# A two-layer hybrid backbone on one core: decay matrices made once per head, SiLU on ScalarE, z gates as a block, and the last weights before each residual norm taken token tile by token tile

## The chip, the cores and the metric

One core of one Trainium2 chip runs the whole program in one launch. The metric is the device time of an execution in microseconds (us). The kernel before takes 1237.73 us, the median of 3 runs (1231.84 to 1239.37).

## The reference, cut to what matters

Two layers act on 384 tokens (128 context tokens, 256 latent tokens of a grid 64 wide) with D = 1024 and 8 heads of 128. Layer 0 mixes tokens with a gated DeltaNet in both directions, layer 1 with HGRN2 in both directions; behind each mixer stand a residual RMS norm, a second norm and a squared-ReLU MLP. All weights are float32.

```python
# layer 0, per direction, chunks of c tokens
qkv = silu(token_conv(qkv, conv_w, grid))          # conv of 5 taps
q, k = l2_normalise(q), l2_normalise(k)
beta = sigmoid(braw); g = -exp(a_log) * softplus(araw + dt_bias)
g = cumsum(g)
decay = exp(where(causal, g[:, None] - g[None, :], -inf))
lower = (k * beta) @ k.T * decay * strict          # tmat = inverse of (1 + lower)
qk = q @ k.T * decay
u, w = tmat @ (v * beta), tmat @ (k * beta * exp(g))
v_new = u - w @ state; o = (q * exp(g)) @ state + qk @ v_new
o = rms_norm(o_fwd + o_bwd, onorm_g) * silu(z); mix = o @ w_out
# layer 1, per direction, chunks of c tokens
b = cumsum(log f); q_in = q * exp(b); k_out = k * exp(-b)
o = causal(q_in @ k_out.T) @ v + q_in @ state
# behind each mixer
x = x + gt1 * rms_norm(mix, g1)
h = rms_norm(x, g2) * (1 + sc2) + sh2
x = x + gt2 * rms_norm(square(relu(h @ w1)) @ w2, g3)
```

## The kernel before

**Tiling.** Tokens stand in three tiles of 128 (`NT` = 3, tile 0 is the context). A float32 product with weights is made of three products of halves: `split` (L898) turns a piece of weights `wr` into a high half `wh` (a cast on ScalarE) and a low half `wl` (a subtraction on VectorE), both of type fp32r, and `mm3` (L918) issues hi·hi, lo·hi and hi·lo. The activations are held transposed as `hhi` and `hlo`. PSUM has 8 banks; tiles named `pj`, `acc`, `pf`, `nat`, `pb`, `po`, `k`, `pad` share them.

**Order of the work.** The functions do not issue instructions; they hand each one to a `Planner` (L431 to L687) with a cost, the tiles that it reads and writes, and the name of its unit (`pl.unit`). The planner then runs a list schedule over PE, VectorE (DVE), ScalarE (ACT), GpSimd (POOL) and the SP queue, with a table of shifts per unit, numbers of buffers per pool and a cost for each form, and writes one fixed order per engine. Every DMA is issued from the SP queue, in the order so found; a DMA that must wait there holds those behind it.

**Stages.** In time: the start (adaLN of the first norm, and the projection of the first weights, `k`); the first mixer, `gdn` (L1236); its output projection `out_proj` (L1090) with the residual norm `postnorm` (L1065) and the next `prenorm` (L1040); `mlp` (L1125); the second mixer `hgrn` (L1605) with its `out_proj`; the second `mlp`. Beside them `ada` (L976) and `ada_rows` (L952) make the modulation vectors.

**First mixer.** `phase1` (L1385) makes, for a head, k by `conv` (L1295: copies, five taps on ScalarE and VectorE, a Tanh on ScalarE and two products on VectorE that make of it twice the SiLU), k·k, and the matrices `PU`. `inverse` (L1418) inverts the 64-token blocks of four heads: the 32-wide diagonal blocks go through DRAM (`du`, `dt`) to a layout in which 31 steps on VectorE solve them all together, and matmuls on quarters of the array (`merge`, L1450) put the rest together. `phase2` (L1488) makes q, v and the gate z of a head and then the outputs. `decay` (L1367) is called by both phases: for each token tile a mask by a 128x256 bf16 matmul with the identity (`maskb`, `identb`), two products of 6 rows (`LR`) on top, and an Exp on ScalarE into `dec`.

**Residual norms.** In `out_proj` the output weights come as four units of 1 MB, (half of the columns) x (half of the rows `kh`); for each unit a loop over three token tiles adds 12 matmuls to `acc`, and in the last unit `postnorm` of a tile follows its 12. In `mlp` the last group (g = 7) of `w2` (L1177) does the same with its two halves. `postnorm` squares both halves of `acc` on ScalarE, raises the sum to the power -0.5 on POOL (`rms`, L1030) and updates `x` on VectorE; `prenorm` squares `x` again, scales it to `xn`, transposes `xn` on PE (`pj`, line 814) and makes `hf`, `hhi` and `hlo`. The first weights of the MLP (`w1_rows`, L1151, PSUM tile `nat`) then run token tile by token tile.

**Second mixer.** In `head` (L1637), `intra` (L1672, called 24 times) fills a 128x256 PSUM tile with zeros by one matmul of `zerob` and then writes blocks into it: per direction one 64x64 product (`A64`), two 32x32 products (`A32`), four 32x32 products (`hQD`, `hKD`).

```python
PE.matmul(pat[:, :256], lhsT=zerob[:, :128], rhs=zerob[:, :256], start=True, stop=True, ...)
for e in range(2):
    PE.matmul(pat[j0:j0 + 64, ...], lhsT=A64k[:, e, :], rhs=A64q[:, e, :], ..., tile_position=(0, j0))
    for hb in range(2): ...   # A32, 32 wide
    for bb in range(4): ...   # KD, 32 wide
```

Of the kernel before, what the change touches and what calls it, by code (L numbers as in the profile page):

```python
# [8 lines left out]
F = mybir.dt.float32  # L9
# [8 lines left out]
D = 1024  # L18
# [6 lines left out]
C_ID, C_SEL, C_TF, C_TB, C_SF, C_SB, C_ONE = 0, 128, 144, 272, 400, 528, 656  # L25
C_HM = 784
# [17 lines left out]
SWITCH = 1036
TICK = 10240 / 3
WINDOW = 3446
SHIFT = {'aoh0': -1315,
 'aopn0': -1765,
 'aopn1': -753,
 'aopn2': 6,  # L50
 'aow0': -66,
 'aow1': 105,
 'aow2': 91,
 'aow3': 243,
 'aow:ld': -320,
# [132 lines left out]
 'hz2': 84,
 'hz3': -246,
 'hz4': -223,  # L190
 'hz5': -369,
 'hz6': -535,
 'hz7': -381,
 'hz:sp': 41,
 'inv0': 376,
 'inv1': 197,
 'k0': 142,
 'k1': 387,
 'k2': -103,
 'k3': -103,  # L200
 'k4': 118,
 'k5': 72,
 'k6': -159,
 'k7': -12,
 'k:ld': -168,
 'k:sp': -484,
 'kk0': -48,
 'kk1': 100,
 'kk2': 8,
 'kk3': -1,  # L210
 'kk4': -88,
 'kk5': 536,
 'kk6': -386,
 'kk7': 561,
 'q0': 108,
 'q1': 47,
 'q2': -283,
 'q3': -54,
 'q4': -177,
 'q5': 328,  # L220
 'q6': -392,
 'q7': 128,
 'q:ld': 78,
 'q:sp': -489,
 'st0': -1339,
 'st1': -1079,
 'st2': -2702,
 'st3': -192,
 'st4': -270,
 'st5': -1125,  # L230
 'st6': -78,
 'st7': -66,
 'v0': -96,
 'v1': -39,
 'v2': 161,
 'v3': -310,
 'v4': -183,
 'v5': 36,
 'v6': -268,
 'v7': -231,  # L240
 'v:ld': -23,
 'v:sp': -349,
 'x': -1361,
 'z0': -467,
 'z1': -85,
 'z2': 193,
 'z3': -435,
 'z4': 339,
 'z5': -273,
 'z6': -30,  # L250
 'z7': 234,
 'z:ld': -146,
 'z:sp': -378}
# [4 lines left out]
ADA = ((675, 63), (1031, 109), (1624, 175), (3306, 321), (4201, 189), (4487, 20), (5276, 1), (5517, 124),  # L258
 (4443, 58), (10707, 169))
BUFS = {'A32': 5,  # L260
 'A64': 7,
 'CR': 5,
 'LR': 3,
 'Zs': 8,
 'ab': 2,
 'acc': 8,
 'adw': 3,
 'am': 4,
 'ar': 7,
 'atm': 4,  # L270
 'att': 5,
 'av': 4,
 'avj': 3,
 'ax': 5,
 'c4': 4,
 'cacc': 3,
 'cbuf': 2,
 'crow': 3,
 'dec': 7,
 'e1': 6,  # L280
 'gate': 5,
 'gr': 5,
 'hE': 3,
 'hEn': 3,
 'hKD': 5,
 'hQD': 5,
 'hel': 7,
 'het': 5,
 'hf': 4,
 'hf0': 1,  # L290
 'hhi': 5,
 'hk': 5,
 'hlo': 8,
 'hsf': 4,
 'inv': 4,
 'k0': 6,
 'k2': 2,
 'kT': 4,
 'ktt': 3,
 'lbo': 5,  # L300
 'lhl': 3,
 'mh': 5,
 'ml': 4,
 'mr': 6,
 'nat': 6,
 'natr': 3,
 'of': 5,
 'ofl': 1,
 'oin': 5,
 'on': 6,  # L310
 'osb': 3,
 'pad': 5,
 'pb': 8,
 'pf': 4,
 'pj': 3,
 'pm': 4,
 'pnt': 3,
 'po': 5,
 'r': 6,
 'rstd': 7,  # L320
 's0': 7,
 's1': 2,
 'sf': 3,
 'sg': 4,
 'sqj': 6,
 'ss': 8,
# [1623 lines left out]
```

## Time and profile before

| | us |
|---|---|
| median of 3 runs | 1237.73 |
| lowest, highest run | 1231.84, 1239.37 |
| span of the profiled execution (first to last instruction) | 1238.8 |
| PE busy in it | 1196.9 |
| VectorE busy | 822.5 |
| ScalarE busy | 626.9 |
| GpSimd busy | 66.4 |

No time other than its span is given for the profiled execution; the span stands 1.1 us above the median. Busy times are sums over instructions of one engine; engines work beside each other. "Idle" of PE is the part of a stretch in which no matmul was in flight. The granted TensorE clock of the execution is 0.971 of full speed in the mean.

### The profile page before, as it was taken

The numbers are of one execution on the slowest core, as the hardware profiler recorded it, in microseconds if no ns is written. First come the engines' busy times: TensorE is split into PE (matmuls) and PEld (weight loads), VectorE is DVE, ScalarE is ACT, GpSimd is POOL, SyncE is SP. The second block draws the span as 40 slices with busy tenths as digits, with TensorE's granted clock in tenths as the row PEclk, the third lists the DMA queues.
The fourth block names the chain that finished last, engine by engine and source line by source line (L and its number), as shares of the span: only waits on it lengthen the run. The fifth ranks groups of instructions, "written<-read, shape, count | busy, mean of one in ns | idle before, by whom it ended". The sixth has DMA issues, their size and how long they took to land.

```text
span 1238.8 us, 20262 instructions
## 1 busy us (share of the span) xinstructions
PE 1196.9 (97%) x7840; PEld 1068.7 (86%) x7840; DVE 822.5 (66%) x1673; ACT 626.9 (51%) x1253; POOL 66.4 (5%) x165
## 2 busy tenths in 40 slices
PE   5999999999998999999998999999998999999997
PEld 3877798999887999999887999998976898998886
DVE  3487997947779999984439856677776963323434
ACT  3364445556646634453327764774665564443432
POOL 1112100000002000000002000000002000000000
PEclk9998996969998999999999999999999999999999
DMA  8864553413234666665336723443334353424322
GB/s 304 289 249 141 205 123 115 135 65 105 88 112 163 233 263 249 231 251 187 129 106 224 230 78 110 127 145 115 113 111 170 139 183 107 140 99 168 137 103 85
DMA packets 76613, 195.89 MB, mean 158 GB/s; under 512 B 24318, under 2 KB 44950, under 8 KB 64486
## 3 DMA queue, kind: packets, MB, share of 16 engines
q1 hardware_dynamic: 76518, 194.61, 45.8%
q8 instruction: 61, 1.00, 0.3%
q14 instruction: 34, 0.28, 0.1%
HBM read 185.31 MB, written 9.27 MB: 157 GB/s over the span
## 4 chain that ended last, share of the span: by engine, by line
PE 93%; DMA 2%; ACT 2%; DVE 1%; POOL 1%; issue 1%; SPq 0%; POOLq 0%; DVEq 0%; ACTq 0%
PE pj L809 35%; PE acc L809 26%; PE pb L809 14%; PE pf L809 8%; PE nat L809 3%; PE po L809 2%; PE pb L814 2%; PE pad L809 2%; PE k L809 1%; DMA wr<-in_gk_dram 1%; DMA cst<-in_consts_dram 1%; POOL rstd L725 1%; DVE hf L736 1%; DMA x<-in_x_sample_dram 1%; ACT xn L774 0%
## 5 line engine op out<-in xcount | busy, mean ns | idle before, releaser
L725 DVE TENSOR_TENSOR wl<-wr,wh 128x1024 fp32r<-128x1024 f32 (+2 forms) x228 | 266.5, 1171 | 241.3 <-ACT wh L779 236.3
L779 ACT CAST wh<-wr 128x1024 fp32r<-128x1024 f32 (+2 forms) x228 | 229.8, 1010 | 385.5 <-PE acc L809 187.7
L809 PE MATMUL pj<-hhi,wh 128*128 128x384 f32 x800 | 270.4, 343 | 1.1 <-ACT hhi L779 1.1
L809 PE MATMUL pj<-hlo,wh 128*128 128x384 f32 x800 | 269.3, 342 | 0.1
L809 PE MATMUL pj<-hhi,wl 128*128 128x384 f32 x800 | 268.2, 341 | 0.0
L809 PEld LDWEIGHTS pj<-hhi,wh 128*128 128x128 f32 x800 | 150.9, 189 | 6.0 <-issue 1.6
L809 PEld LDWEIGHTS pj<-hhi,wl 128*128 128x128 f32 x800 | 150.9, 189 | 3.5 <-DVE cacc L730 0.4
L809 PEld LDWEIGHTS pj<-hlo,wh 128*128 128x128 f32 x800 | 151.0, 189 | 2.7 <-DVE hlo L725 0.3
L809 PE MATMUL acc<-wl,mh 128*128 128x512 f32 x384 | 149.6, 390 | 0.0
L809 PE MATMUL acc<-wh,ml 128*128 128x512 f32 x384 | 148.9, 390 | 0.0
L809 PE MATMUL acc<-wh,mh 128*128 128x512 f32 x384 | 141.7, 391 | 0.0
L730 DVE SCALAR_TENSOR_TENSOR avj<-av,cb 128x1024 bf16<-128x1024 f32 x112 | 134.1, 1219 | 3.2 <-DMA av<-in_wv_dram 2.8
L809 PEld LDWEIGHTS acc<-wh,ml 128*128 128x128 f32 x384 | 72.1, 188 | 14.5
L809 PEld LDWEIGHTS acc<-wl,mh 128*128 128x128 f32 x384 | 72.1, 188 | 14.3
L809 PEld LDWEIGHTS acc<-wh,mh 128*128 128x128 f32 x384 | 71.7, 188 | 13.4
L809 PE MATMUL pf<-wh,hhi 128*128 128x384 f32 x192 | 65.5, 344 | 2.8 <-ACT hhi L779 2.8
L809 PE MATMUL pf<-wl,hhi 128*128 128x384 f32 x192 | 66.1, 344 | 0.0
L809 PE MATMUL pf<-wh,hlo 128*128 128x384 f32 x192 | 65.3, 342 | 0.6 <-DVE hlo L725 0.6
L730 DVE SCALAR_TENSOR_TENSOR cacc<-cb,cw,cacc 128x392 f32<-128x392 f32 x96 | 58.1, 617 | 0.5 <-ACT cacc L774 0.2
L809 PE MATMUL pad<-ar,csil 128*32 128x256 f32 x320 | 31.7, 431 | 13.3 <-DVE csil L740 8.9
L774 ACT ACTIVATE hE<-pb 128x512 f32<-128x512 f32 x48 | 28.9, 603 | 23.1 <-PE pb L809 19.5
L809 PEld LDWEIGHTS pf<-wh,hhi 128*128 128x128 f32 x192 | 36.1, 188 | 4.3 <-ACT hhi L779 3.5
(255 smaller groups left out, 2004.7 us busy)
## 6 DMA issues: line engine op xcount, KB each, us to landing
wr<-in_w_dram SPq DMA_DIRECT2D x64, 1024.0 KB
av<-in_wv_dram SPq DMA_DIRECT2D x56, 512.0 KB
ar<-in_wa_dram SPq DMA_DIRECT2D x40, 512.0 KB
wr<-in_gq_dram SPq DMA_DIRECT2D x14, 1024.0 KB
wr<-in_hfi_dram SPq DMA_DIRECT2D x16, 768.0 KB
wr<-in_hqz_dram SPq DMA_DIRECT2D x8, 1024.0 KB
wr<-in_gout_dram SPq DMA_DIRECT2D x4, 1024.0 KB
wr<-in_hout_dram SPq DMA_DIRECT2D x4, 1024.0 KB
```

The lines of the kernel that those rows point to most:

```text
L725: self._go(lambda: self.r.tensor_tensor(fix(out), fix(in0), fix(in1), op), _n(out), [out], [in0, in1], rate, base=base)
L730: self._go(lambda: self.r.scalar_tensor_tensor(fix(out), fix(in0), fix(scalar), fix(in1), op0, op1, **{k: fix(v) for k, v in kw.items()}), ...
L736: self._go(lambda: self.r.tensor_scalar(*[fix(x) for x in args]), _n(out), [out], [in0, s1, s2], rate, base=None if self.e == "V" else 160 ...
L774: self.pl.add("S", lambda: self.r.activation(fix(out), fix(in_), func, **{k: fix(v) for k, v in kw.items()}), cost, w, [x for x in (in_, b ...
L779: self.pl.add("S", lambda: self.r.copy(fix(out), fix(in_)), cost, [out], [in_])
L809: self.pl.add("PE", lambda: self.r.matmul(fix(out), lhsT=fix(lhsT), rhs=fix(rhs), start=start() if callable(start) else start, stop=stop, ...
L814: self.pl.add("PE", lambda: self.r.transpose(fix(out), fix(in_), fix(ident)), 108.0, [out], [in_, ident], kind="tr")
```

## The change

1. **Decays once.** `decay` of a head runs once, into a tile of all three token tiles, and is stored to DRAM (`dd`). `phase1` of heads 4 to 7 reads it back as `dre`, `phase2` of all heads as `att`, where one product of 768 columns replaces three of 256.
2. **SiLU on ScalarE** in `conv` and for z in the first mixer, in place of Tanh and products on VectorE; the constants of the norms lose their factor 4.
3. **z gates as a block.** The weights `gq` are packed anew (k of heads 4 to 7, all z, then q and v per head); the eight z blocks run ahead of `phase2`, each stored to `zd` and read back (`zl`) where a head ends.
4. **Last weights by token tile.** In `out_proj` and in the last group of `mlp` (and for head 0 of the second mixer) both last units are split first, four pieces resident at once (`split4`, the fourth in the extra tiles `xh`, `xl`), and each token tile then takes its 24 matmuls in a row.
5. **`intra` 32 wide.** Four zero matmuls of 32x96 that cover the part above the diagonal blocks, all products 32 columns wide, each on its own quarter of the array's columns.
6. **`inverse`**: other layouts of `du` and `dt`, so that 24 transposes of 32x32 blocks become 4 large ones and there are fewer DMAs, with 24 more small ScalarE copies.
7. The small inputs come in one packed DMA (`sml`), `cst` in one, states in one DMA for both directions.
8. The planner's costs, buffer numbers and shifts are other numbers.

```diff
-        def decay(h, after):
-            dts = []
+        def decay(h):
+            pl.unit(f"d{h}")
+            e = tl("L3", "dec", 3, [128, NT, 2, 128])
             for n in range(NT):
                 px = pb()
-                e = tl("L1", "dec", 3, [128, 256])
...
-                S.activation(e, px[:, :256], AF.Exp)
-                dts.append(e)
-            return dts
+                S.activation(e[:, n].rearrange("p d t -> p (d t)"), px[:, :256], AF.Exp)
+            DM.dma_start(out=dd[h], in_=e.rearrange("p n d t -> p (n d t)"))
+            return e
+        def gate(h, p):
+            zs = tl("L1", "zs", ZS, [128, T])
+            S.activation(zs, p, AF.Silu)
+            DM.dma_start(out=zd[h], in_=zs)
...
-            t = tl("L1", "th", 2, [128, 392])
-            S.activation(t, acc, AF.Tanh, scale=0.5)
-            V.scalar_tensor_tensor(out[:, 0:128], t[:, 0:128], 1.0, acc[:, 0:128], ALU.add, ALU.mult)
-            V.scalar_tensor_tensor(out[:, 128:384].rearrange("p (r c) -> p r c", r=4),
...
+            S.activation(out[:, 0:128], acc[:, 0:128], AF.Silu)
+            S.activation(out[:, 128:384].rearrange("p (r c) -> p r c", r=4), sub(acc, 130, [[66, 4], [1, 64]]),
+                         AF.Silu)
...
-            dec = decay(h, qT)
             pkq = pb()
-            att = tl("L3", "att", 2, [128, NT, 2, 128])
+            att = decay_of(h, "att")
...
+        dts = [decay(h) for h in range(4)]
         for h in range(4):
             pl.unit(f"k{h}")
-            phase1(h, k0[1 + h])
+            phase1(h, k0[1 + h], dts[h])
...
+        for h in range(H):
+            pl.unit(f"z{h}")
+            gate(h, get(4 + h))
         for h in range(H):
-            phase2(h, get, 4 + 3 * h)
+            phase2(h, get, 12 + 2 * h)
```

```diff
+        pl.unit(f"{u}ow2")
+        pcs = split4([load(w[2 + kh], 4) for kh in range(2)], [128, 2, 512])
+        for n in range(NT):
+            pl.unit(f"{u}ow2")
+            pst[n][1] = ps("acc", 6)
+            for k in range(KC):
+                hi, lo = pcs[k // 2]
+                mm3(pst[n][1], hT["hi"][k][:, tsl[n]], hT["lo"][k][:, tsl[n]], hi[:, k % 2, :], lo[:, k % 2, :],
+                    k == 0, k == KC - 1)
+            pl.unit(f"{u}opn{n}")
+            postnorm(n, pst[n], x[n], gate)
...
+                for bb in range(4):
+                    PE.matmul(pat[32 * bb:32 * bb + 32, 32 * bb + 32:32 * bb + 128], lhsT=zerob[:, :32],
+                              rhs=zerob[:, :96], start=True, stop=True, tile_position=(0, 32 * bb),
+                              skip_group_check=True, after=[KD])
+                jobs = []
+                for e in range(2):
+                    j0, i0 = 64 * (1 - e), 64 * e
+                    for c in range(2):
+                        jobs.append((j0 + 32 * c, e, i0, 64, A64k[:, e, 32 * c:32 * c + 32], A64q[:, e, :]))
```

**How the order moves.** PE, one `intra` of a later head; `hQD`, `hKD`, `A` are the operands, `pb` the PSUM tile. Before:

```order
L809 LDWEIGHTS zerob
L809 MATMUL pb_7512<-zerob 128x256
L809 MATMUL pb_7512<-A_1527_7483,A_1528_7487 64x64
L809 MATMUL pb_7512<-A_1529_7490,A_1530_7493 32x32 x2
L809 MATMUL pb_7512<-hQD_7497,hKD_7503 32x32 x4
```

The last three rows stand there once more for the other direction. After the change:

```order
L926 MATMUL pb_7151<-A_1424_7132,A_1425_7137 32x64 x4
L926 MATMUL pb_7151<-A_1426_7139,A_1427_7146 32x32 x4
L926 MATMUL pb_7144<-vtt_6925,het_7108 128x128
L926 MATMUL pb_7164<-vtt_6925,het_7108 128x128 x2
L926 LDWEIGHTS zerob
L926 MATMUL pb_7151<-zerob 32x96
...
L926 MATMUL pb_7151<-hQD_7149,hKD_7162 32x32 x8
```

The 64-wide rows are gone and the zeros stand four times (the middle ones are left out); an `intra` is now mostly two visits to the narrow shape with other work between them, 47 in all for 24 calls.

PE, the residual norm behind the first mixer; `acc` takes output weights, `pj<-...xn` are the transposes of `prenorm`, `nat` the first MLP products. Before, `xn_4607`, `xn_4634` and `xn_4676` are token tiles 0, 1 and 2:

```order
L809 MATMUL acc_4526<-wh_4534,hlo_4011 128x512
L814 MATMUL pj_4643<-cst,xn_4607 128x128 x4
L814 MATMUL pj_4653<-cst,xn_4607 128x128 x4
L809 MATMUL nat_4686<-wh_4655,hhi_4680 128x256
L814 MATMUL pj_4691<-cst,xn_4634 128x128 x4
L814 MATMUL pj_4707<-cst,xn_4634 128x128 x4
L814 MATMUL pj_4718<-cst,xn_4676 128x128 x4
L814 MATMUL pj_4726<-cst,xn_4676 128x128 x4
L809 MATMUL nat_4686<-wl_4714,hhi_4680 128x256
```

After, they are `xn_4356`, `xn_4433` and `xn_4490`:

```order
L926 MATMUL acc_4382<-xh_4305,hlo_3975 128x512
L932 MATMUL pj_4468<-sml,xn_4433 128x128 x4
L926 MATMUL nat_4494<-wh_4418,hhi_4426 128x256
L926 MATMUL nat_4494<-wl_4428,hhi_4426 128x256
L926 MATMUL nat_4494<-wh_4418,hlo_4442 128x256
L932 MATMUL pj_4508<-sml,xn_4490 128x128 x4
L932 MATMUL pj_4514<-sml,xn_4356 128x128 x4
L932 MATMUL pj_4527<-sml,xn_4433 128x128 x4
L932 MATMUL pj_4536<-sml,xn_4490 128x128 x4
```

The first transposes of tile 0 and the first three `nat` products have moved up among the `acc` products of tile 2; behind the last `acc` product three `nat` products stand ahead of the first transposes of tile 2, and the second halves of tiles 0 and 1 stand behind those.

The SP queue in the first mixer after the change, where `dd` and `zd` are the new DRAM tiles and `wr` is a unit of weights (before, no row of this kind stands there but for `du` and `wr`):

```order
L943 DMA dre_1249<-dd 128x768
L943 DMA dre_1257<-dd 128x768
L943 DMA dre_1316<-dd 128x768
L943 DMA inv_1321<-du_89 96x1024
L943 DMA wr_1327<-in_gq_dram 128x2048
L943 DMA dre_1359<-dd 128x768
L943 DMA zd<-zs_1350 128x384
L943 DMA att_1388<-dd 128x768
```

Over the whole program the SP queue has 404 rows where it had 431, and 36 of them are the new stores and read-backs (8 `dd`, 8 `zd`, 4 `dre`, 8 `att`, 8 `zl`). Matmuls per kind: `LR` 96 to 48, `maskb` 48 to 24, `zerob` 24 of 256 columns to 96 of 96 columns; products of `acc`, `pj`, `pf`, `nat` are as many as before. VectorE has 1561 rows before and 1466 after, ScalarE 1107 and 1131, with five more table loads.

## Rows read from the trace of the kernel before

**Rows 1.** The page, busy time, share of the span and instructions of each engine.
```profile
PE 1196.9 (97%) x7840; PEld 1068.7 (86%) x7840; DVE 822.5 (66%) x1673; ACT 626.9 (51%) x1253; POOL 66.4 (5%) x165
```

**Rows 2.** The page, chain of work that ended last, by engine.
```profile
PE 93%; DMA 2%; ACT 2%; DVE 1%; POOL 1%; issue 1%; SPq 0%; POOLq 0%; DVEq 0%; ACTq 0%
```

**Rows 3.** Windows by stage: us, busy by engine, granted clock, DMA share, GB/s.
```profile
0.00:62.00 62.00, 46.80 (x315) 35.39 (x315) 23.95 (x62) 20.99 (x41) 7.04 (x23) 0.97 0.87 297
62.00:376.50 314.50, 312.67 (x2470) 271.70 (x2469) 245.39 (x657) 171.96 (x453) 28.66 (x79) 0.92 0.42 137
376.50:394.50 18.00, 12.55 (x69) 10.94 (x69) 17.11 (x34) 12.66 (x30) 4.70 (x10) 0.81 0.09 32
...
652.90:668.00 15.10, 9.98 (x47) 7.43 (x46) 14.10 (x30) 14.22 (x37) 7.78 (x15) 0.89 0.68 225
...
951.00:975.00 24.00, 16.55 (x99) 15.09 (x98) 22.29 (x42) 14.95 (x37) 6.45 (x14) 0.93 0.37 137
```

**Rows 4.** Waits of PE: waiting <- waited for: us in total, times, longest.
```profile
PE pj L814 <- DVE xn L736: 10.4, 6, 5.0
```

**Rows 5.** PE timeline of one head's decays: start, length, instruction.
```profile
90.76 0.27 PE L809 MATMUL pb<-maskb,identb 128*128 128x256 bf16 x1
...
91.17 0.28 PE L809 MATMUL pb<-maskb,identb 128*128 128x256 bf16 x1
```

**Rows 6.** Lines of PE by form: count | busy, mean ns | idle before.
```profile
L809 PE MATMUL pb<-maskb,identb 128*128 128x256 bf16 x48 | 13.9, 289 | 0.1
```

**Rows 7.** PE timeline of one `intra` of the second mixer.
```profile
716.97 0.28 PE L809 MATMUL pb<-zerob 128*128 128x256 bf16 x1
717.19 0.48 PE L809 MATMUL pb<-A,A 128*64 128x64 f32 x4
717.46 0.23 PE L809 MATMUL pb<-hQD,hKD 128*32 128x32 f32 x2
...
717.69 0.48 PE L809 MATMUL pb<-A,A 128*64 128x64 f32 x4
...
718.20 0.49 PE L809 MATMUL po<-s,hQD 128*128 128x128 f32 x2
```

**Rows 8.** PE timeline behind the first mixer; in brackets the idle time before.
```profile
375.90 0.39 PE L809 MATMUL acc<-wl,hhi 128*128 128x512 f32 x1
376.13 0.39 PE L809 MATMUL acc<-wh,hlo 128*128 128x512 f32 x1
377.94 1.11 PE L814 MATMUL pj<-cst,xn 128*128 128x128 f32 x8 [1.42 <-DVE xn L736]
381.74 0.58 PE L809 MATMUL nat<-wh,hhi 128*128 128x256 f32 x1 [2.69 <-ACT hhi L779]
...
386.67 0.56 PE L809 MATMUL nat<-wl,hhi 128*128 128x256 f32 x1
```

**Rows 9.** Timelines of ACT, DVE and POOL in the same stretch.
```profile
376.95 0.58 ACT L774 ACTIVATE sqj<-acc 128x512 bf16<-128x512 f32 x1
...
375.54 1.41 DVE L730 SCALAR_TENSOR_TENSOR x<-pnt,rstd,x 128x512 f32<-128x512 f32 x2 [0.29 <-POOL rstd L725]
...
384.51 0.88 DVE L736 TENSOR_SCALAR xn<-x,rstd 128x512 f32<-128x512 f32 x2 [0.44 <-POOL rstd L725]
...
377.89 0.43 POOL L725 TENSOR_TENSOR rstd<-ss 128x1 f32<-128x1 f32 x1
378.40 0.55 POOL L725 TENSOR_TENSOR rstd<-rstd,nhalf 128x1 f32<-128x1 f32 x1
```

**Rows 10.** Windows in the first mixer where the granted clock is low.
```profile
183.00:206.00 23.00, 22.24 (x316) 20.60 (x314) 17.30 (x50) 10.95 (x26) 1.08 (x6) 0.57 0.52 152
247.00:268.00 21.00, 20.05 (x263) 19.21 (x264) 6.47 (x16) 8.31 (x20) 0.14 (x2) 0.51 0.28 99
```

**Rows 11.** Waits of the SP queue: us in total, times, longest.
```profile
SPq L825 <- DVE wl L725: 563.1, 91, 19.1
...
SPq L825 <- DMA od<-of: 7.6, 6, 1.5
```

More of the change, by code (lines that the diff above doesn't have):

```diff
@@ new lines @@
+M_CC, M_ID, M_SEL, M_C0, M_DT, M_CW, M_OG, M_ADB, M_LG = 0, 16, 144, 146, 170, 172, 292, 294, 406
+M_COLS = 438
+RESERVE = {'A32': 26,
+ 'A64': 73,
+ 'CR': 13,
+ 'HC': 4,
+ 'LR': 2,
+ 'PU': 0,
+ 'T64': 7,
+ 'Zs': 28,
+ 'ab': 18,
+ 'acc': 1,
+ 'adw': 2,
+ 'am': 35,
+ 'ar': 2,
+ 'atm': 54,
+ 'att': 19,
+ 'av': 2,
+ 'avj': 2,
+ 'ax': 5,
+ 'c1': 40,
+ 'cacc': 0,
+ 'cb': 2,
+ 'cbuf': 3,
+ 'crow': 58,
+ 'cvec': 2,
+ 'dec': 22,
+ 'dre': 11,
+ 'e1': 29,
+ 'gate': 13,
+ 'gp': 13,
+ 'gr': 16,
+ 'hE': 7,
+ 'hEn': 10,
+ 'hKD': 7,
+ 'hQD': 9,
+ 'hel': 65,
+ 'het': 1,
+ 'hf': 8,
+ 'hf0': 3,
+ 'hhi': 20,
+ 'hk': 10,
+ 'hlo': 9,
+ 'hsf': 11,
+ 'inv': 30,
+ 'iv': 21,
+ 'k0': 7,
+ 'k2': 0,
+ 'kT': 37,
+ 'ktt': 0,
+ 'lbo': 2,
+ 'lhl': 17,
+ 'mh': 16,
+ 'ml': 31,
+ 'mr': 13,
+ 'mst': 23,
+ 'nat': 4,
+ 'natr': 21,
+ 'of': 0,
+ 'ofl': 0,
+ 'oin': 47,
+ 'on': 60,
+ 'ors': 11,
+ 'osb': 0,
+ 'pad': 2,
+ 'pb': 2,
+ 'pf': 1,
+ 'pj': 2,
+ 'pm': 5,
+ 'pnt': 5,
+ 'po': 3,
+ 'qT': 0,
+ 'r': 36,
+ 'rstd': 30,
+ 'rsu': 34,
+ 's0': 4,
+ 's1': 68,
+ 'sf': 0,
+ 'sg': 11,
+ 'sqj': 17,
+ 'ss': 24,
+ 'ss2': 34,
+ 'sso': 48,
+ 'ssq': 45,
+ 'swt': 2,
+ 'tb': 3,
+ 'th': 16,
+ 'vT': 0,
+ 'vtt': 2,
+ 'w': 62,
+ 'w2': 70,
+ 'wh': 0,
+ 'wl': 0,
+ 'wr': 22,
+ 'x': 22,
+ 'xh': 13,
+ 'xl': 13,
+ 'xn': 25,
+ 'zl': 1,
+ 'zs': 2}
@@ L295 @@
+ 'gp': 4,
+ 'gr': 8,
+ 'hE': 4,
+ 'hEn': 8,
+ 'hKD': 7,
+ 'hQD': 7,
+ 'hel': 7,
+ 'het': 4,
+ 'hf': 8,
+ 'hf0': 2,
+ 'hhi': 3,
+ 'hk': 6,
+ 'hlo': 6,
+ 'hsf': 2,
  'inv': 4,
- 'k0': 6,
+ 'iv': 6,
+ 'k0': 9,
  'k2': 2,
[L298 to L305, printed above, removed]
+ 'kT': 6,
+ 'ktt': 8,
+ 'lbo': 6,
+ 'lhl': 7,
+ 'mh': 6,
+ 'ml': 5,
+ 'mr': 3,
+ 'mst': 4,
+ 'nat': 5,
  'natr': 3,
- 'of': 5,
- 'ofl': 1,
- 'oin': 5,
+ 'of': 6,
+ 'ofl': 2,
+ 'oin': 6,
  'on': 6,
- 'osb': 3,
@@ L455, in place, with add @@
         self.nplace += 1
-    def add(self, eng, call, cost, writes, reads, func=None, dma=None, kind=None, grid=None, rows=1.0):
+    def add(self, eng, call, cost, writes, reads, func=None, dma=None, kind=None, grid=None, rows=1.0, geo=None):
         op = Op()
@@ L537, in run @@
         dma_free = 0.0
+        lanes = []
         actset = None
@@ L1596, in gdn @@
         get = blocks(a["gq"])
+        for h in range(4, 8):
+            decay(h)
         for h in range(4, 8):
```

907 lines of the change are left out of this document (461 added, 446 removed).

## The prediction

> **What bounds the kernel now.** I read the page first. PE is busy 1196.9 us, 97% of the span, VectorE 66%, ScalarE 51% [rows 1], and the chain that ended last is PE for 93% of the span [rows 2]. So only two kinds of saving count: time in which PE works (or switches) and time in which PE has nothing. The windows by stage show where the second kind is [rows 3]: 15.2 us in the start (62.00 less 46.80), 1.8 in the whole first mixer (314.50 less 312.67), and 5.45, 5.12 and 7.45 us, 18.0 together, behind the first mixer, behind the first MLP's end and behind the second mixer. The waits of PE put 10.4 us in six waits on `xn` of VectorE, the input of the transposes in those norms [rows 4]. In the first mixer VectorE is busy 245 us of 314.5, but PE hardly waits there, so work taken from VectorE alone buys nothing in that stage. The granted clock is another matter: 0.92 in the mean there, against 1.00 later; two stretches of 44 us together stand near 0.5, the lower of the two levels (1.2 of 2.4 GHz), although PE is busy through 42 of them [rows 10].
>
> **Part 1, the decays.** One tile of decays starts at 90.76 and the next at 91.17 [rows 5]: 0.41 to 0.42 us of PE for the mask and its two small products. There are 48 such tiles [rows 6], 24 go: 24 x 0.42 = **-10.1 us**, all of it PE time in a stage with no idle time to spare. Bounds: -7 (half of the masks' busy 13.9 us [rows 6], if the small products hide wholly) and -13 (24 x 0.55, mask 0.27 and products 0.28 one behind the other).
> What comes in their place is DMA: 8 stores and 12 read-backs of 393 KB, and for z 8 stores and 8 read-backs of 197 KB. At 137 GB/s and a DMA share of 0.42 [rows 3], the stage has room; 11 MB is some 80 us of the present rate spread over 314 us. I cost it at nothing on the path; what hides it is that the order issues the first read-backs well before the heads that use them. If that cover is gone it is the rival on the slower side below.
>
> **Part 2, `intra`.** One call runs from 716.97 to 718.20, 1.23 us [rows 7]. In it the zeros take 0.22 (to 717.19), each 64-wide round 0.27 or so (717.19 to 717.46), each group of 32-wide products 0.23 (717.46 to 717.69), and round and group come twice. After the change no shape alternates: one round of A products on four quarters in place of two (0.27), the eight diagonal products and the zeros in some 0.25, since a whole group of ten short records takes 0.23 with the switch to the next shape in it, and one more switch because the call now makes two visits, some 0.12 by half of such a group. That is 0.65 us: 1.23 - 0.65 = 0.58, times 24 calls = **-13.9 us**. Bounds: -17 if a call is one visit (0.12 less each), and +3 if nothing runs side by side (20 instructions at 0.07, a quarter of a 64-wide round, are 1.40 us).
> The page "TensorEngine Tiling (Array Packing)" of the Trainium skill, section Instruction Overhead, speaks against this part: each matmul has an overhead of about 60 cycles, so that splitting what is short already gains little. At 25 ns (60 cycles at 2.4 GHz) the 36 passes of the 16 products and four zeros would take 0.9 us by an estimate from that page, and the part would be worth 8 us. The group of ten records in 0.23 us shows less than that per record, so I stay with the rows; what would follow is the first rival.
>
> **Part 3, last weights by token tile.** Before, behind the first mixer, the last `acc` product starts at 376.13, the transposes run in pieces from 377.94, and steady `nat` products start at 386.67 only [rows 8]. With 12 products each, the three tiles' postnorms come 2.8 us apart and share ScalarE, VectorE and POOL, so that tile 2's `xn` is scaled at 384.51 [rows 9], 8.4 us after the last product starts. A product starts 0.23 behind the one before (375.90, 376.13). After the change each tile has 24 of them, so tiles come 5.5 us apart and tiles 0 and 1 are through when tile 2 ends; its chain runs alone. From [rows 9] it has: `sqj` 0.58 and its accumulator read, some 0.8; POOL's sum and power 0.43 + 0.55, 1.0; two `x` updates 1.4; the second square of `x` 0.8; POOL again 1.0; half of `xn` 0.45: **5.4 us**. The order shows that PE still stops for it: behind the last `acc` product there are only four transposes and three `nat` products (about 0.8 us), then the transposes of tile 2, and the second halves of tiles 0 and 1 behind them. So the stall shrinks by 8.4 - 5.4 = 3.0 us and does not go. Three places: **-9 us**. Bounds: 0, if the new order makes the wait as long by other means, and -20, the idle time of 18.0 and some fill, if the wait were gone. The end of the second MLP gains nothing: there only tile 2's chain counts, and it stands behind the last product as before.
>
> **Part 4, at about nothing.** SiLU and the bulk transposes take some 30 us from VectorE and add small ScalarE copies and five table loads; PE hardly waits for either engine in that stage and ScalarE is busy 172 of 314.5 us [rows 3]: 0, bounds -2 and +3. The order has some 20 more switches of PE to the shape of the adaLN products; at 0.1 us each: **+2**. The start: thirteen small DMAs fewer, but some transfers moved ahead in a stretch whose DMA share is 0.87: 0, bounds -4 and +4.
>
> **Sum.** 1238.8 - 10.1 - 13.9 - 9 + 2 = 1207.8 us of span. The span of the profiled execution is all that is given of it, and it stands 1.1 above the median of the runs, so the forecast is **1206.5 us**, 2.5% less. Its own range, from the bounds taken halfway, is 1195 to 1217.
>
> **Rivals.**
> First, short products gain little: `intra` is limited by instructions and not by shapes, so that part brings 0 to -8 us. For it: each record has some fixed cost, and there are now more rows. Against it: ten records in 0.23 us [rows 7]. The time is 1206.5 + 10 = 1217.
> Second, the stalls at the norms nearly vanish (-20 in place of -9), because VectorE and ScalarE have no more splits to do there and the wait on `xn` is the only long one [rows 4]. Against it: the order keeps tile 2 ahead of work that is ready. The time is 1195.
> Third, the clock: a part of the 44 us near 0.5 comes back up, as the small products of the decays, which are bf16 with 6 rows, leave the mixer and the z blocks, long runs of 384 columns, fill other places. They lose 20 us (23 x 0.43 and 21 x 0.49); two thirds of it are 13: 1193. Against it: the same z blocks then no longer stand between the chains of `phase2`, so stretches may fall that were at full clock; I hold both about as likely, and the other sign is in the upper range.
> Fourth, slower: the SP queue. It issues in one order and stops for a DMA that waits. A store that was read back has cost 7.6 us in six waits, 1.27 each [rows 11]; 36 new DMAs of this kind at 1.27 are 46 us of holding, in a stage where the queue already brings weights behind waits for `wl`, 563.1 us in all. If it falls into the order badly, the weight unit that stands behind is late and PE starves: 1206.5 + 46 = 1252. It decides when the hold is longer than PE can work on what is resident, two units of two blocks each. Against it: PE has waited for no weights in this mixer (1.8 us idle of 314.5), and the stores stand well ahead of most read-backs.
> The page "DMA: Bandwidth & Descriptors" of the Trainium skill, section Latency and other measured facts, names a fixed cost of about 2 us for a DMA. By it the 36 would hold for 72 us, an estimate, where the row gives 46; both weigh for this rival, and neither says how much of it reaches PE.
>
> **How the numbers follow.** Forecast 0.47, first rival 0.17, second 0.16, third 0.11, fourth 0.09. A measurement of this kernel can tell about 1% from no change, so faster means under 1225.4 and slower over 1250.1. The forecast, the second and third rival are faster with nearly all of their weight (0.71 of 0.74), of the first 0.12 of 0.17; the fourth is half slower and half between, since a part of the hold may be hidden. That gives 0.83 faster, 0.12 same, 0.05 slower. The range, with 1 in 10 left out at each side: 1178 (second and third together, and the lower bounds of parts 1 and 2) to 1231 (the first rival with no gain at the norms and something of the fourth).
>
> **What would show it.** In the profile of the changed kernel: `maskb` x24 and the first mixer's stage about 10 us shorter, at a like clock; one `intra` at 0.65 us of PE in its two visits, and the second mixer's stage about 14 us shorter; from the last `acc` product to the first transposes of tile 2 some 5 to 6 us, with PE's waits on `xn` still there but fewer; the tail as before. The forecast is wrong if PE waits on `wh` or `wl` in the first mixer with the SP queue held by `dre` or `att`, if the short products take 0.07 each one after the other, or if the mean granted clock of the first mixer moves by more than 0.02.

## The result, and the profile after

The changed kernel takes 1250.38 us in the median of 4 runs (1248.31 to 1252.60) against 1238.18 beside it: a ratio of 1.0113 (95% interval [1.0081, 1.0144], as in the brackets below), slower by 1.1%. The forecast was 1206.5 with a range up to 1231, so it was wrong in sign, by 44 us. The profiled execution has a span of 1249.1 us.

The page of the kernel after, busy times and the chain of waits by engine:

```profile
PE 1195.8 (96%) x7936; PEld 1054.9 (84%) x7936; DVE 796.9 (64%) x1578; ACT 635.0 (51%) x1282; POOL 66.0 (5%) x156
...
PE 80%; DVE 7%; ACT 6%; DMA 4%; issue 2%; POOL 1%; SPq 0%; DVEq 0%; POOLq 0%; ACTq 0%
```

VectorE lost 26 us, as meant, and PE's busy time is 1.1 us less than in [rows 1], where the forecast took some 24 us of work from it. PE's share of the chain fell from 93% [rows 2] to 80%: VectorE, ScalarE and DMA now end waits that count. The windows by stage of the kernel after (columns as in [rows 3]) show where:

```profile
0.00:67.00 67.00, 54.12 (x371) 38.57 (x372) 30.61 (x69) 27.43 (x51) 7.21 (x22) 1.00 0.93 341
67.00:378.80 311.80, 295.77 (x2349) 257.41 (x2348) 236.07 (x600) 183.30 (x485) 27.75 (x76) 0.93 0.56 179
378.80:390.80 12.00, 5.94 (x26) 4.99 (x26) 10.47 (x20) 7.08 (x18) 4.47 (x7) 0.67 0.70 242
390.80:662.10 271.30, 271.30 (x1402) 244.92 (x1401) 174.75 (x249) 117.30 (x180) 3.56 (x10) 1.00 0.52 181
...
676.80:959.30 282.50, 280.32 (x2316) 250.27 (x2314) 217.74 (x486) 167.69 (x340) 12.47 (x21) 1.00 0.41 142
```

The same stages of the kernel before, cut at the same events:

```profile
0.00:61.70 61.70, 46.50 (x314) 35.33 (x315) 23.95 (x62) 20.69 (x41) 7.04 (x23) 0.97 0.87 296
61.70:376.30 314.60, 312.77 (x2472) 271.76 (x2470) 245.19 (x657) 172.06 (x452) 28.54 (x78) 0.92 0.42 137
376.30:387.00 10.70, 5.91 (x27) 4.50 (x27) 9.81 (x20) 10.29 (x27) 4.82 (x11) 0.70 0.07 29
387.00:655.30 268.30, 267.65 (x1404) 243.63 (x1402) 196.24 (x291) 116.75 (x178) 2.20 (x8) 1.00 0.56 205
...
666.80:952.70 285.90, 285.31 (x2169) 260.96 (x2167) 204.68 (x455) 171.26 (x334) 8.97 (x16) 1.00 0.42 136
```

In the first mixer PE is busy 17.0 us less, but idle for 16.0 us where it was 1.8. A second profile of the kernel after (run 2 below) has it idle for 9.4 us, at a lower clock:

```profile
66.50:376.60 310.10, 300.74 (x2349) 260.36 (x2347) 235.92 (x600) 183.54 (x485) 27.70 (x75) 0.91 0.57 180
```

The first MLP, whose products are the same and run at full clock in both, takes 271.3 us where it took 268.3. The start is 5.3 us longer: 30 more adaLN products stand in it, and 24 products of 384 columns, some 4.2 us of work, that stood in the first mixer before.

To add this up, each interval between the starts of two neighbouring matmuls was set against the median interval of its form at full clock in the kernel before. What equals it is work; what a lower granted clock explains is clock; a small excess of a wide product is pace; an excess under 0.2 us (changes of shape, mostly) is small; one over that is a stall. Two profiles of each kernel, in us:

| | work | clock | pace | small | stalls | sum |
|---|---|---|---|---|---|---|
| before | 1088.2, 1088.2 | 25.7, 18.2 | 5.2, 5.4 | 52.1, 53.2 | 51.9, 50.3 | 1223.1, 1215.2 |
| after | 1066.1, 1066.4 | 21.8, 24.2 | 14.3, 14.3 | 55.9, 54.8 | 75.6, 71.6 | 1233.8, 1231.2 |
| difference of the means | -22.0 | +1.1 | +9.0 | +2.7 | +22.5 | +13.3 |

What counts as work and what as small depends on the median that is taken for a form which mostly stands beside others; the two together fell by 19.3 us. So the work went about as forecast (24 us of it were expected to go), and two things gave it back: stalls (+22.5) and a slower pace of the wide products (+9). The stalls of the first mixer are 17.0 and 17.2 us before, 35.0 and 30.3 after; those of the start rose by some 4.

The waits of PE in the kernel after (waiting <- waited for: us in total, times, longest):

```profile
PE pj L932 <- DVE xn L851: 7.6, 5, 2.4
PE pb L926 <- ACT Zs L898: 6.1, 4, 4.0
PE nat L926 <- ACT hhi L894: 5.9, 4, 3.2
PE pb L926 <- ACT dec L889: 3.4, 1, 3.4
```

Left out is one wait in the start, 8.1 us for `csil`, which was 8.9 before. At the norms `xn` has 7.6 us for 10.4 [rows 4], and the waits on `hhi` behind it changed little (2.7 of `nat` and 2.8 of `pf` before, 5.9 of `nat` now). In the first mixer the waits for `Zs`, copies of the inverse on ScalarE, rose from 1.7 to 6.1, and one for `dec`, also on ScalarE, is new. The longest two, on PE and then on ScalarE:

```profile
102.47 0.49 PE L926 MATMUL pb<-kT 128*128 128x128 f32 x2 [3.37 <-ACT dec L889]
...
254.26 0.95 PE L926 MATMUL pb<-inv,Zs 32*32 32x32 f32 x14 [3.96 <-ACT Zs L898]
```

```profile
96.94 1.28 ACT L889 ACT_TABLE_LOAD   x1
98.23 0.31 ACT L889 ACTIVATE kT<-cacc 128x128 f32<-128x128 f32 x1
98.66 2.07 ACT L894 COPY tb<-PU 32x384 f32<-32x384 f32 x4
100.74 1.28 ACT L889 ACT_TABLE_LOAD   x1
102.04 1.76 ACT L889 ACTIVATE dec<-pb 128x256 f32<-128x256 f32 x6
...
252.17 1.04 ACT L894 CAST wh<-wr 128x1024 fp32r<-128x1024 f32 x1 [4.86 <-DMA wr<-in_gq_dram]
...
253.73 0.48 ACT L898 ACTIVATE Zs<-pb 32x384 f32<-32x384 f32 x1
```

At 97 us a SiLU of k and four copies stand among the Exps of the decays, with a table load before and behind; PE's next product waits until a `pb` tile that `dec` reads is free. At 247 us a cast of weights waits 4.9 us for its DMA and holds the short copy `Zs` behind it. Neither engine is busy all the time; here it is the order that holds. In the second profile the order is the same, but PE waited 0.46 us for that `dec`, and 2.86 for that `Zs`: its clock was lower around the first place (0.70 for 0.79 over 40 us), so that it came later by itself. Whether taking these two holds away gives the time back is tried below.

### The profile page after: what moved, and what is told of

Same layout as the page of the kernel before. It is cut to its first block, busy times and chain, and to the rows that moved or that the text cites. A ratio compares the mean times of both kernels' runs of the same rounds, so it can differ in the third digit from the quotient of the medians.

```text
span 1249.1 us, 20371 instructions
## 1 busy us (share of the span) xinstructions
PE 1195.8 (96%) x7936; PEld 1054.9 (84%) x7936; DVE 796.9 (64%) x1578; ACT 635.0 (51%) x1282; POOL 66.0 (5%) x156
## 4 chain that ended last, share of the span: by engine, by line
PE 80%; DVE 7%; ACT 6%; DMA 4%; issue 2%; POOL 1%; SPq 0%; DVEq 0%; POOLq 0%; ACTq 0%
PE pj L926 30%; PE acc L926 26%; PE pb L926 7%; PE pf L926 7%; PE nat L926 3%; PE pad L926 2%; PE k L926 2%; PE po L926 2%; PE pb L932 1%; PE pj L932 1%; DMA inv<-dt 1%; DVE avj L845 1%; ACT wh L894 1%; DVE cacc L845 1%; ACT L889 1%
## 5 line engine op out<-in xcount | busy, mean ns | idle before, releaser
L840 DVE TENSOR_TENSOR wl<-wr,wh 128x1024 fp32r<-128x1024 f32 (+2 forms) x223 | 260.8, 1171 | 292.9 <-ACT wh L894 282.6
L894 ACT CAST wh<-wr 128x1024 fp32r<-128x1024 f32 (+2 forms) x223 | 224.5, 1008 | 392.8 <-PE pj L926 199.2
L926 PE MATMUL pj<-hlo,wh 128*128 128x384 f32 x800 | 272.6, 344 | 0.0
L926 PE MATMUL pj<-hhi,wl 128*128 128x384 f32 x800 | 272.0, 344 | 0.1
L926 PE MATMUL acc<-wh,ml 128*128 128x512 f32 x372 | 145.8, 395 | 0.0
L926 PE MATMUL acc<-wl,mh 128*128 128x512 f32 x372 | 145.3, 395 | 0.0
L845 DVE SCALAR_TENSOR_TENSOR avj<-av,cvec 128x1024 bf16<-128x1024 f32 x112 | 134.3, 1217 | 1.9 <-DMA av<-in_wv_dram 1.5
L845 DVE SCALAR_TENSOR_TENSOR cacc<-cb,sml,cacc 128x392 f32<-128x392 f32 x96 | 59.1, 619 | 3.8 <-ACT cacc L889 3.1
L926 PE MATMUL pad<-ar,csil 128*32 128x256 f32 x320 | 36.4, 428 | 8.6 <-DVE csil L855 8.1
L840 DVE TENSOR_TENSOR ml<-mr,mh 128x384 fp32r<-128x384 f32 x56 | 30.6, 556 | 12.3 <-ACT mh L894 8.1
```

Of the source, the lines that this page charges most:

```text
L840: self._go(lambda: self.r.tensor_tensor(fix(out), fix(in0), fix(in1), op), _n(out), [out], [in0, in1], rate, base=base)
L845: self._go(lambda: self.r.scalar_tensor_tensor(fix(out), fix(in0), fix(scalar), fix(in1), op0, op1, **{k: fix(v) for k, v in kw.items()}), ...
L894: self.pl.add("S", lambda: self.r.copy(fix(out), fix(in_)), cost, [out], [in_])
L926: self.pl.add("PE", lambda: self.r.matmul(fix(out), lhsT=fix(lhsT), rhs=fix(rhs), start=start() if callable(start) else start, stop=stop, ...
```

## The experiments

The variants of before keep its whole order: the planner plans the old instructions, and only what a planned instruction issues is replaced. So one part of the change is tried without the new order.

**1 and 2. Both kernels again.** No edit.

> The kernel before once more, profiled on the same chip as the next runs. In the two traces so far a product of 512 columns starts 227 ns behind the one before it in the kernel before and 232 ns in the changed kernel, everywhere in the program, 1440 times (about 9 us over all wide products). Theory A, the chip or the day: here it is the same number as in the changed kernel run beside it. Rival B, the program: 227 here and 232 there.

> The changed kernel once more, beside the kernel before. Ratio to the kernel before 1.008 to 1.014 by what was measured. Theory A: its 512-column products start at the same interval as those of the kernel before in this job, so that the 9 us of slower wide products are no part of the change, and the stalls (about +24 us against the kernel before) carry the result. Rival B: 232 ns against 227.

Before: 1238.45 us, 1.0003 [0.9976, 1.0031]. After: 1249.27 us, 1.0116 [1.0076, 1.0156]. Executions of before range from 1230 to 1245 us, and its two profiles differ by 7.5 us in the clock column of the table alone: one profile of one kernel does not settle a few microseconds.

**3. `intra` 32 wide, in one visit, in before's order.**

```diff
-matmul(zerob 128x256); per direction: A 64x64; A 32x32 x2; hQD,hKD 32x32 x4
+matmul(zerob 32x96) x4; then, in before's places, A 32x64 x2; A 32x32 x2; hQD,hKD 32x32 x4
```

> The kernel before with its order kept instruction by instruction; only intra is changed: four zero products of 32x96, all others 32 columns wide, one visit per call. My theory (0.58 us a call in the prediction, 0.70 with one visit): 14 to 17 us less than the kernel before, one call about 0.55 to 0.65 us of PE. Rival, limited by instructions: 0 to 8 us less.

1237.99 us, 1.0019 [0.9992, 1.0046]: no gain in the total. Yet one call takes 0.53 us, from the zeros to the next shape, for 1.23 in [rows 7]:

```profile
717.93 0.23 PE L814 MATMUL pb<-zerob 128*32 128x96 bf16 x4
...
718.46 0.49 PE L811 MATMUL po<-s,hQD 128*128 128x128 f32 x2
```

The second mixer is 277.9 us long where it was 286. What took it back is the pace of everything else: the first MLP, ahead of the edit, takes 271.6 us and the second 271.8, as in the kernel after. That called for runs 5, 6, 9 and 11.

**4 and 7. Decays once, in before's order.** Each head's decays are stored to DRAM and read back into two extra buffers for `phase2`; the second set of masks, products and Exps is left out. In the first of the two the read-back is issued too early and fetches, for part of the heads, decays that are not theirs; in the second it is issued behind the previous use of its buffer.

```diff
+DMA dd[h, n] <- dec            # behind each Exp of phase1
+DMA back[h % 2] <- dd[h]       # in phase2
-maskb, LR, LR, Exp; att = pkq * dec
+att = pkq * back[h % 2]
```

> The kernel before with its order kept; phase2 makes no decays: 24 masks, 48 small products and 24 Exps are gone, the decays of phase1 are stored and read back per head in one DMA, issued with the head's first instruction. My theory: 10 us less (24 x 0.42). Rival, the SP queue: 8 read-backs and 24 stores hold weights and PE waits; no gain, or up to 10 us more.

> As b_decay, with the read-back of a head behind its conv of q, so that it stands behind the stores and behind the use two heads earlier. b_decay took 1233.64 against 1236.57 with read-backs that came too early. My theory of the prediction: 24 x 0.42 = 10 us less. Rival: PE gets back only 3 to 5 us, since what waited behind the decays waits still (stall in the first mixer up by 5 us or more).

1233.64 us, 0.9971 [0.9955, 0.9986], and 1232.37 us, 0.9963 [0.9937, 0.9988]. In the second, work in the first mixer is 243.9 us for 253.8, the -10 that was forecast, and its stalls are 21.6 for 17.0. So about half of the term reaches the end (4.3 us between the medians of run 7 and of before beside it, 1.5 to 7.8 by the interval). Beside the first profile of before, whose clock column in this stage is about the same, the first mixer is 6.3 us shorter, 308.3 us for 314.6. The longest new wait of PE is 1.8 us for `att`, the product of VectorE that follows the read-back.

**5, 6 and 9. What sets the pace.** Run 5 adds 60 short products at the start of before; run 6 makes one of the 24 `intra` calls 32 wide, run 9 is run 6 again.

```diff
+for i in range(60): matmul(pad 32x32)        # run 5
-parts=[...]
+parts=None if cnt[0] else [...]              # runs 6 and 9: the first call only
```

> The kernel before with 60 more short products (32x32, 120 more records on PE) in the start, where PE waits for data; their results are overwritten. The wide products were 227 ns apart in the kernel before and 232 in each kernel with more PE instructions. Theory L, the length of PE's program: 232 here. Rival F, the new forms of intra: 227 here.

> The kernel before with intra 32 columns wide in the first of its 24 calls alone (5 instructions, some 7 records more). Theory L: 227 ns between wide products, since the program is hardly longer. Rival F: 232, if the form alone does it; the first MLP runs ahead of that call, so that nothing it leaves behind in one execution could slow that.

> The same kernel as b_one once more, loaded anew. It had wide products 232 ns apart and 1247 us, with one call of 24 changed; b_pad with more products had 227. Theory P, the pace is a property of the built program: 232 again. Rival R, it is drawn anew at each load: 227 as likely as not.

Single executions: 1240.36, 1247.42 and 1247.36 us. One call of 24 makes the whole program slower by some 9 us, again in the second job; 60 extra products elsewhere do not. The wide products, by form, in run 5 (before has the same row) and in run 6 (count | busy, mean ns | idle before):

```profile
L809 PE MATMUL acc<-wh,ml 128*128 128x512 f32 x384 | 148.9, 390 | 0.0
```

```profile
L811 PE MATMUL acc<-wh,ml 128*128 128x512 f32 x384 | 150.7, 395 | 0.0
```

The mean of this row is 390 or 391 ns in some programs, 395 ns in the others, and nothing between; by their starts, products of 512 columns follow each other at 227 or at 232 ns, through the whole of a program.

**8. The copies of the inverse on GpSimd**, in the kernel after.

```diff
-S.copy(tb[0][s], P[1][s, :, s])
+nc.gpsimd.tensor_copy(tb[0][s], P[1][s, :, s])     # 24 copies in all
```

> The changed kernel in its own order, with the 24 small copies of inverse on GpSimd and not on ScalarE. In the changed kernel PE waits 6.1 us for Zs and 3.4 us for dec, both of ScalarE, while ScalarE makes these copies (0.5 us each). Theory: 3 to 6 us less, the waits on Zs under 4 us and on dec under 2. Rival: nothing, since the wait passes to GpSimd, to VectorE or to weights.

1242.35 us, 1.0064 [1.0035, 1.0093], 6 to 8 us less than the kernel after. But its wide products have the mean of 391 ns, the first mixer's stalls are 34.5 us, and PE's waits for `Zs` are still 6.0 us. The gain is the pace; the theory that the 24 copies crowd ScalarE falls.

**10. Decays once and `intra` 32 wide together, in before's order** (edits of runs 3 and 7).

> The kernel before, in its order, with b_intra and b_decay2 together. From the stages: intra 8 to 10 us (mixer 2 was 277.9 us in b_intra, 286 in the kernel before), decays 4 to 5 us as b_decay2 measured. If its wide products are 227 ns apart: 1222 to 1225 us, faster than both kernels; if they are 232 ns apart: 1231 to 1235.

1220.78 us, 0.9842 [0.9802, 0.9882]: faster than both kernels. Its windows of the first and of the second mixer:

```profile
61.70:369.10 307.40, 300.62 (x2400) 266.38 (x2398) 244.41 (x657) 164.15 (x429) 29.40 (x78) 0.92 0.50 161
...
659.60:934.40 274.80, 273.66 (x2337) 251.89 (x2335) 203.44 (x455) 171.19 (x334) 9.58 (x16) 1.00 0.43 141
```

Its work is 1064.5 us, as little as in the kernel after; its pace column is 5.3 and its stalls are 56.0. So the 30 us between it and the kernel after are none of work: 9 us are pace and 16 to 20 are stalls, which came with the rest of the change and its order. Of the 23.7 us of work that it has less than before, 17.9 came off the span (1220.9 us for 1238.8) and 19.6 off the median by its ratio (14.6 to 24.5).

**11. `intra` 32 wide with the 60 extra products** (edits of runs 3 and 5).

> b_intra with the 60 short products of b_pad in the start: same forms, same order, another program. Theory P (pace of the program, whatever the form): it may come out at 227 ns, and then intra is worth 8 to 10 us, 1226 to 1229. If it is 232 again, near 1238 as b_intra; then the form of intra may still be the cause.

1230.54 us, 0.9931 [0.9909, 0.9953]. The pace is the faster one again, with every `intra` 32 wide:

```profile
L811 PE MATMUL acc<-wh,ml 128*128 128x512 f32 x384 | 149.0, 390 | 0.0
```

Its second mixer:

```profile
665.80:942.50 276.70, 274.35 (x2337) 251.91 (x2336) 203.48 (x456) 171.07 (x334) 8.88 (x15) 1.00 0.43 140
```

So `intra` in one visit is worth 8 to 9 us, and its form does not set the pace.

**12. The norm chains first.** In the kernel after, the splits and adaLN reductions that stand among the last norm chain (10, 10 and 9 instructions at three places) go behind it.

```diff
-done = [... wl, xn, wl, pnt, x, x, hlo, xn, wl, xn ...]
+done = [... xn, pnt, x, x, hlo, xn, xn, wl, wl, wl ...]
```

> The changed kernel; at the three residual norms the weight splits and adaLN products that stand on ScalarE and VectorE among the chain of the last token tile are moved behind it (10, 10 and 9 instructions). Theory: that chain (7.7 us from the last product to xn at the first norm, where 5.4 were predicted) is held by them; it falls to 5.5 to 6.5 and each norm by 1 to 2 us, 3 to 6 us in all. Rival: no change, since POOL and the tiles' own instructions hold it.

1249.29 us, 1.0104 [1.0064, 1.0143], at the faster pace (391 ns): what the pace gave, some 9 us, was lost elsewhere. The chain at the first norm did shorten as expected, to 6.4 us from the last product (374.84) to `xn`:

```profile
381.21 0.88 DVE L875 TENSOR_SCALAR xn<-x,rstd 128x512 f32<-128x512 f32 x2 [1.12 <-POOL rstd L864]
```

But the norm stages are 12.9, 16.5 and 12.6 us for 12.0, 14.7 and 11.3, PE waits 6.8 us for `wl` at `nat`, and the first MLP has 7.1 us of stalls for 0.3: the splits that were moved are what PE wants next.

**13 to 15. The two holds on ScalarE.** In the kernel after. Run 13: the SiLUs and copies at 97 us behind seven Exps, two table loads fewer. Run 14: the cast at 247 us behind four copies of the inverse. Run 15: both.

```diff
-Silu kT, copy tb x4, Exp dec x6, Silu kT x2, Exp dec
+Exp dec x7, Silu kT, copy tb x4, Silu kT x2          # runs 13, 15
-cast wh, copy T, Zs, PU, PU, Zs, ..., Zs, PU
+copy T, Zs, PU, PU, Zs, ..., Zs, PU, cast wh         # runs 14, 15
```

> The kernel after with one stretch of ScalarE's order changed: the last two SiLUs of k (head 7) and the four copies of the first inverse stand behind seven Exps of the decays instead of among them, so that two table loads (1.28 us each) go. Theory 'queue order on ScalarE' (the stalls of PE in the first mixer come from short work that stands behind other work in ScalarE's order): the 3.4 us wait of PE for dec at 99 us goes, and less than 1 us of it comes back at the kT products behind; first mixer 2 to 4 us shorter than in the kernel after, at a like clock. Rival 'the chain moves' (the inverse or the kT products become late by as much): the idle time of PE between 90 and 125 us stays within 1 us of the kernel after's.

> The kernel after with one cast moved: the cast of q's weights of head 5, which waits 4.9 us on ScalarE for its DMA at 247 us, stands behind the four copies of the inverse that it held. Theory 'queue order on ScalarE': the 4.1 us wait of PE for Zs at 250 us goes, the following stretch keeps its clock, and the first mixer is 3 to 6 us shorter. Rival 'the weights are late': PE waits as long for the weights a few microseconds later (the products of head 5), and the first mixer is within 1 us of the kernel after's at a like clock.

> Both of these moves in one kernel. Theory 'queue order on ScalarE': stalls of the first mixer 6 to 8 us less than in the kernel after, and its time 1241 to 1245 us at the same pace of the wide products (1233 to 1236 if this program has the faster pace). Rival 'it comes back elsewhere': 1247 to 1251 us (1238 to 1242 at the faster pace).

1238.75 and 1247.49 us in single executions, and 1250.67 us, 1.0110 [1.0045, 1.0175], for both. Run 13 has the faster pace, 14 and 15 the slower one. The waits of PE at the two places in run 15:

```profile
103.24 0.94 PE L947 MATMUL pb<-kT 128*128 128x128 f32 x6 [1.45 <-ACT dec L910]
106.24 0.80 PE L947 MATMUL pb<-kT 128*128 128x128 f32 x2 [1.96 <-ACT kT L910]
108.64 1.22 PE L947 MATMUL pb<-kT 128*128 128x128 f32 x4 [1.28 <-ACT kT L910]
...
258.88 0.29 PE L947 MATMUL pb<-T,PU 64*64 64x64 f32 x2 [0.96 <-ACT T L915]
263.18 0.91 PE L947 MATMUL pb<-T,PU 64*64 64x64 f32 x12 [0.28 <-DMA T<-dt]
267.38 0.73 PE L947 MATMUL pb<-PU,Zs 64*64 64x64 f32 x9 [1.90 <-ACT Zs L919]
```

The 3.4 us wait became three of 4.7 together, for the SiLU that now comes later; the 4.0 us wait became three of 3.1. The stalls of the first mixer are 32.9, 32.4 and 33.2 us for 35.0 and 30.3 in the two profiles of the kernel after. For run 15 the rival is right: its time is the one that the rival gave, the holds can be moved, and something else is late instead. Single profiles can't show a gain of 2 or 3 us here, since those two differ by 5 in this column. The order of ScalarE at these two places is not what costs the 13 to 18 us.

## Why the prediction was wrong, point by point

**Part 1, decays, -10.1.** Right in PE's work: `maskb` stands 24 times, and 243.9 for 253.8 us in run 7 is the term. Wrong was to take all of it as path ("all of it PE time in a stage with no idle time to spare"). Run 7 kept 4 to 5 us of the 10 by its median, some 6 by its first mixer, and its stalls rose by 4.4. A likely reason is that taking a product from PE leaves the inputs of the next one as late as they were; no run shows that by itself.

**Part 2, `intra`, -13.9.** Right in the work, as counted above: 265.2 to 251.3 us in the second mixer. But that stage shrank by 3.4 us only, from 285.9 to 282.5. Its small excesses rose by 5.2. The step that failed is the price of the second visit, 0.12 us per call, with nothing for the products beside it. The kernel after shows one call like this:

```profile
749.76 0.34 PE L926 MATMUL pf<-wh,hlo 128*128 128x384 f32 x1
749.94 0.34 PE L926 MATMUL pf<-wh,hhi 128*128 128x384 f32 x1
750.21 0.38 PE L926 MATMUL pb<-A,A 128*32 128x64 f32 x16
750.51 0.45 PE L926 MATMUL pf<-wl,hhi 128*128 128x384 f32 x1
750.80 0.62 PE L926 MATMUL pb<-HC,lhl 128*128 128x512 f32 x2
...
751.53 0.23 PE L926 MATMUL pb<-zerob 128*32 128x96 bf16 x4
751.58 0.30 PE L926 MATMUL pb<-hQD,hKD 128*32 128x32 f32 x16
751.81 0.73 PE L926 MATMUL pb<-HC,lhl 128*128 128x512 f32 x2
```

The two visits take 0.30 and 0.28 us, 0.58 together. But a `pf` product of 384 columns, 0.18 us from start to start otherwise (749.76 to 749.94), takes 0.27 ahead of the first visit and 0.29 behind it: 0.2 us of a visit lie in its neighbours. Waits came to 4 us more and the pace to 1.3. In one visit and at the faster pace (run 11) the part is worth 9.2 us of the stage (276.7 us), although the call itself went from 1.23 to 0.53 us, so the bound of -17 was out of reach as well. The first rival, that short products are limited by instructions, is not what happened: run 3 has its 36 records in 0.53 us. One after the other, with the overhead of about 60 cycles each that the section Instruction Overhead of the Trainium skill's page "TensorEngine Tiling (Array Packing)" names, they would have taken the 0.9 us estimated in the prediction; the measurement decides. Whether that overhead is smaller here or runs side by side on the four quarters, no run tells. Neighbours and visits are what has to be priced.

**Part 3, last weights by token tile, -9.** Wrong: nothing came of it. The norm stages less their work were 7.7, 7.3 and 8.3 us and are 9.2, 7.3 and 8.0. The step that failed is "its chain runs alone". In the kernel after, behind the last `acc` product at 378.56 (timelines of ScalarE, VectorE and POOL):

```profile
377.82 1.99 ACT L894 CAST wh<-wr 128x1024 fp32r<-128x1024 f32 x2
379.70 0.60 ACT L889 ACTIVATE sqj<-acc 128x512 bf16<-128x512 f32 x1
...
380.29 1.22 DVE L840 TENSOR_TENSOR wl<-wr,wh 128x1024 fp32r<-128x1024 f32 x1
381.42 0.68 DVE L840 TENSOR_TENSOR pnt<-acc,gate 128x512 f32<-128x512 f32 x1
...
384.55 1.21 DVE L840 TENSOR_TENSOR wl<-wr,wh 128x1024 fp32r<-128x1024 f32 x1
386.48 0.88 DVE L851 TENSOR_SCALAR xn<-x,rstd 128x512 f32<-128x512 f32 x2 [0.71 <-POOL rstd L840]
...
384.72 1.09 POOL L840 TENSOR_TENSOR rstd<-ss 128x1 f32<-128x1 f32 x1 [0.44 <-ACT xn L889]
385.89 0.55 POOL L840 TENSOR_TENSOR rstd<-rstd,nhalf 128x1 f32<-128x1 f32 x1
```

The chain of tile 2 takes 7.9 us (378.56 to 386.48), where 5.4 were forecast and 8.4 read before. The square waits behind two casts of the next weights until 379.70, `pnt` behind a `wl`, and POOL's sum and power take 1.63 and 1.64 us, not 1.0. That too comes from the splits: the sum takes 0.19 us in run 12, where VectorE stands idle beside it, and here 1.09 (384.72 to 385.81), to just behind the end of the `wl` on VectorE (385.76). And PE waited for tile 1 first (1.57 us for its `xn`, 2.25 for `hhi`), which the forecast had through by then. Run 12 shows both halves: with the splits out of its way the chain takes 6.4 us, and the splits can't simply leave.

**Part 4, at nothing, and the fourth rival.** This is where the forecast lost most. "PE hardly waits for either engine in that stage", read from the kernel before, was taken to hold for another order of the stage. It did not: 13 to 18 us more of stalls came there, some 4 at the start. The fourth rival had a slower kernel, by another mechanism: PE was to starve for weights behind the new DMAs. One wait has that form (the cast at 252.17, which holds `Zs`), and the DMA share of the stage rose from 0.42 to 0.56; but the largest wait of PE on it is 4.0 us (2.9 in run 2), run 14 left 1 us of it without fewer stalls in the stage than run 2 has, and no wait of PE is put down to a new read-back. The SP queue did stand still for the new DMAs, for 28 us of this stage (11.7 for `dec`, 11.4 for `zs`, 4.9 for their stores) of the 46 that were priced, and PE did not starve by it. The third rival, the clock, did nothing (+1.1 us between the means). The +2 us for the switches of the adaLN products were not measured by themselves.

**Not foreseen at all: the pace**, +9 us, a property of the built program as far as the repetitions show. Without it the kernel after would be at about 1241 us, as runs 8 and 13 are: a large part of the 1.1% is this luck of the build, but the missing gain of 2.5% is not.

**The range.** The upper bounds of the prediction's parts lie 3.1, 16.9, 9, 3 and 4 us over its terms. Taken halfway they add up to 18 us, so its own range would have ended at 1224 us, not at 1217; the result lies above either.

**What stays open.** Which of z as a block, SiLU on ScalarE, the new inverse and the new order brings the first mixer's stalls was not separated: these parts share one planned order, and each alone would be planned into another. Runs 8, 13, 14 and 15 show only what does not remove them. The heavier DMA traffic was not tried alone either; run 10, with a share of 0.50 in that stage, has 22.6 us of stalls there.

## What to carry to other kernels

Where the bounding engine has no idle time, work that is taken from it need not come off the time in full: here about half to four fifths of it did (runs 7, 11 and 10), probably because the producers are as late as before. When a change also replaces the order of the program, price the order apart: try the parts that cut work inside the old order first, since that was worth 1.6% here while the whole change cost 1.1%. And a chain is alone on its engines only if nothing else is queued ahead of it there; read that from the order of every engine that it passes, not of PE alone.

## What the hardware showed beyond that

Wide products keep one of two paces for a whole program: 512 columns from start to start in 227 or 232 ns at full clock (means of 390 or 391, and 395 ns, by form), 9 us in total here. Before and after, each run twice, and run 6 with its repetition kept theirs. Two kernels of one job on one chip differed in it, so it is not the chip; run 6 has the same tiles as before, run 5 more PE instructions than run 6 (7960 for 7847), and run 11 the same `intra` as run 3, so neither the placement of data, the length nor that form sets it. Where the instructions themselves lie is not known. Runs 13 and 15, which differ in one moved cast on ScalarE, have different paces. What of the built program decides it stays open; a comparison of two builds within 1% should look at this row first:

```profile
L947 PE MATMUL acc<-wh,ml 128*128 128x512 f32 x372 | 144.3, 391 | 0.0
```

```profile
L947 PE MATMUL acc<-wh,ml 128*128 128x512 f32 x372 | 145.8, 395 | 0.0
```

The first is run 13, the second run 15.

GpSimd's one-column sums at the norms take 0.19 us, or longer beside VectorE: in the first profiles of both kernels and in run 12 every one over 0.2 us, up to 1.09, ends 0.05 us behind an instruction of VectorE that was in progress. A chain through GpSimd has VectorE's order in it too.
